# Sums of weights made by accumulating DMAs, and a fourth pair of the gate and up products in sevens

## The chip, the cores and the metric

The kernel runs on one core of a Trainium2 chip. The metric is the device time of one execution in microseconds (us); several executions are timed and the median is compared. Beside the times there is a profile of one execution. The core has TensorE (matmuls, in the profile PE, its weight loads PEld), VectorE (DVE), ScalarE (ACT), GpSimd (POOL) and SyncE (SP), which here issues nearly all DMAs; 16 DMA engines move the data.

## The reference

One decoder layer on 256 tokens of width 2048, in float32: a gated feed-forward half layer, two parallel token mixers, a second feed-forward half layer, and a gated embedding, with a layer norm behind each. The change touches the two feed-forward half layers alone:

```python
def swiglu(x, w_gu, w_down):
    g, u = jnp.split(x @ w_gu, 2, axis=-1)
    return (jax.nn.silu(g) * u) @ w_down

h = layer_norm(alpha * h + 0.5 * swiglu(h, w_ffn1_gu[i], w_ffn1_down[i]), ln_g[i, 0], ln_b[i, 0])
...
h = layer_norm(alpha * h + 0.5 * swiglu(h, w_ffn2_gu[i], w_ffn2_down[i]), ln_g[i, 2], ln_b[i, 2])
```

The inner width is 5632, so the weights of one half layer are 2048 x 11264 (gate and up) and 5632 x 2048 (down), 92 MB and 46 MB.

## The kernel before

**Matmuls in three parts.** Every float32 operand is split into a high part (ScalarE casts it, L90) and a low part (VectorE subtracts, L91). A product is three matmuls of 128x128 against 128x512: low x high, high x high, high x low (`Sum.add`, L286 to L288).

**Weights come in chunks** of 128 x 1024 floats, 512 KB, by one DMA of SP (`Chunk`, L104). For gate and up the columns are taken in 11 blocks j of 512; in a block the 16 rows of 128 inputs form 8 pairs p, and each pair has a chunk for gate (n = 0) and one for up (n = 1). Half a chunk holds the weights of one of the pair's two input rows. For the down product the 44 input rows form 22 pairs, and the output is made in two halves of 2 x 512 columns.

**Singles and sevens.** A pair is a 2 x 2 block product: two halves of the tokens, two input rows, two output columns, so eight products. As two `Single`s it takes 8 products of 3 matmuls, 24 in all. As one `Seven` it takes 7, 21 matmuls, by a scheme of Strassen's kind. For that the four weights b11, b21 (first chunk) and b12, b22 (second chunk) are combined:

- t1 = b11 + b12, t3 = b12 + b22 (tile u; L162, L163)
- t2 = b11 + t3, t4 = t2 + b21 (tile v; L164, L165)

VectorE makes the four sums, each 128 x 512. Then the first chunk, b22, u and v are split into high and low parts, 3.5 tiles of 128 x 1024. The sums of the inputs are made once (`seven_forms`), and `seven_common` folds the four shared results behind a block. The last seven of a block takes its products in another order, so that these results are ready early. In gate and up, the pairs 0, 1 and 2 of blocks 1 to 10 are sevens, block 0 has singles alone: 30 sevens a half layer. In the down product the pairs of four groups are taken: 4 sevens in the first half, 8 in the second.

**The order of the work is written out by a planner.** `plan` lists all singles and sevens in order. `fill()` runs when a unit is done and writes the next instructions: it makes (splits) a loaded unit while less than 45 matmuls of made units stand ahead (`ahead`), and loads the next while less than 90 stand ahead in all (`far`). Each class says how many slots its load takes (`loads`), how many a make needs free (`makes`), how many it keeps (`keeps`), and its matmuls (`time`). A slot is one of 46 tiles of 4 KB a partition that weights share with activations; `slots_for_weights` says how many the weights may have, 24 in most of gate and up, and 18 to 30 in the tight parts of the down product. All engines run this one order; an instruction waits only for its operands and for its slot to be given back. In the before kernel GpSimd has no DMA.

Of the kernel before, what the change touches and what calls it, by code (L numbers as in the profile page):

```python
# [8 lines left out]
F32 = mybir.dt.float32  # L9
# [3 lines left out]
ALU = mybir.AluOpType  # L13
PSUM = bass.MemoryType.PSUM

P = 128
S = 256
# [15 lines left out]
HELD_PAIRS = 3  # L33
SLOTS = 46

SEVEN = (0, 1, 2)

SEVEN_DOWN = (6, 7, 8, 9)

# [8 lines left out]
def layer(ctx: ExitStack, tc: tile.TileContext, io):  # L48
    nc = tc.nc
    sync, act, dve, pool, pe = nc.sync, nc.scalar, nc.vector, nc.gpsimd, nc.tensor  # L50
# [14 lines left out]
    def slot(shape, dt, name):  # L65
        return slots.tile(shape, dt, tag="slot", name=name)
# [8 lines left out]
    def chunk_of(key):  # L75


        name, at = key[0], key[1:]
        if name.endswith("_gu"):
            j, gu, c = at  # L80
            w = io[name][2 * j : 2 * j + 2, gu, c // 2, :, c % 2 * 2 : c % 2 * 2 + 2, :]
            return w.rearrange("g p k n -> p g (k n)")
        if name[-1] == "2":
            j, c = at
            w = io[name[:-1]][j : j + 2, c // 2, :, c % 2 * 2 : c % 2 * 2 + 2, :]
            return w.rearrange("g p k n -> p g (k n)")
        return io[name][at]

    def split(dst_hi, dst_lo, src, lo_engine=None):
        act.copy(dst_hi, src)  # L90
        (lo_engine or dve).tensor_tensor(dst_lo, src, dst_hi, ALU.subtract)  # L91

    class Chunk:
# [18 lines left out]
        def make(self):  # L112
            self.make_hi()
            split(self.hi, self.lo, self.raw)
# [10 lines left out]
    class Single:  # L125


        loads, makes, keeps, time = 1, 2, 2, 12
# [4 lines left out]
        def load(self, **how):  # L133
            self.chunk = Chunk(self.key, **how)
# [4 lines left out]
    class Seven:  # L139
# [1 line left out]

        loads, makes, keeps, time = 2, 6, 7, 21

        def __init__(self, key, other):
            self.key, self.other = key, other

        def load(self):
            self.a, self.b = Chunk(self.key), Chunk(self.other)  # L150

        def make(self):
            a, b = self.a, self.b
            nm = a.name
            b11, b21, b12, b22 = a.of(a.raw, 0), a.of(a.raw, 1), b.of(b.raw, 0), b.of(b.raw, 1)
            u, v = (slot([P, 2, 512], F32, w + nm) for w in "uv")

            def shaped(x):
                return x.rearrange("p (g n) -> p g n", g=2) if a.paired else x

            t1, t3, t2, t4 = (shaped(x) for x in (u[:, 0], u[:, 1], v[:, 0], v[:, 1]))
            dve.tensor_tensor(t1, b11, b12, ALU.add)  # L162
            dve.tensor_tensor(t3, b12, b22, ALU.add)  # L163
            dve.tensor_tensor(t2, b11, t3, ALU.add)  # L164
            dve.tensor_tensor(t4, t2, b21, ALU.add)  # L165

            def parted(name, x):
                hi, lo = (slot([P, 2, 512], F32R, w + name + nm) for w in "hl")
                split(hi, lo, x)
                return [(hi[:, e], lo[:, e]) for e in range(2)]  # L170

            a.make()
            self.b11, self.b21 = a.columns(0), a.columns(1)
            both = slot([P, 2, 512], F32R, "b" + nm)
            self.b22 = both[:, 0], both[:, 1]
            split(shaped(both[:, 0]), shaped(both[:, 1]), b22)
            self.t1, self.t3 = parted("u", u)
            self.t2, self.t4 = parted("v", v)

# [199 lines left out]
    def plan_tokens(key, n_k, nk=2):  # L379
        for c in range(n_k // nk):  # L380
            plan.append(Single(key + (c,)))
# [279 lines left out]
    def gu_units(j):  # L661
        if j == 0:
            return [("P", p) for p in range(KD // 2)]
        plain = [("P", p) for p in range(KD // 2) if p not in SEVEN]
        out = plain[: len(plain) - len(SEVEN)]
        for a, p in zip(SEVEN, plain[len(plain) - len(SEVEN) :]):
            out += [("S", a), p]
        return out

    def gu_keys(name, j):  # L670
        return lambda n, p: (name + "_gu", j, n, p)
# [18 lines left out]
    def plan_ffn(name):  # L690
        for j in range(KF // 4):
            block_units(gu_units(j), gu_keys(name, j))
        first, second, held = down_units()
        block_units(first, down_keys(name, 0))
        block_units(second, down_keys(name, 1))
        plan.extend(Single(down_keys(name, 1)(n, p)) for n in range(2) for p in held)

    def ffn(name, i, ht, norm, keep, residual, keepers, away):
# [27 lines left out]
        for j in range(KF // 4):  # L726
            pg, pu = banks(f"{name}g{j}"), banks(f"{name}u{j}")
            units = gu_units(j)
            plain = len(units) - sum(kind == "S" for kind, p in units)
            n_of = {(0, 0): KD, (0, 1): KD, (1, 0): KD, (1, 1): KD}  # L730
# [13 lines left out]
            def before(u, j=j, offset=KD // 2 - len(units)):  # L744
# [8 lines left out]
                if j == 0 and u == 7:  # L753
                    for g in sorted({p // 2 for p in SEVEN}):
                        hi, lo = (slot([P, 8, P], F32R, f"{name}f{w}{g}") for w in "hl")
# [539 lines left out]
    with tc.manual_schedule():  # L1295
# [8 lines left out]
        for blk in range(4):  # L1304
            plan_tokens(("w_pg", blk), KD)
        kept = sorted({p // 2 for p in SEVEN})
        norm = ffn("f1", 0, ht, None, x_parts, x_columns, (), rows[0])
# [106 lines left out]
```

## Time and profile before

| | us |
|---|---|
| median of 3 runs | 2328.96 (2327.64 to 2329.99) |
| the profiled execution, its own time | 2328.84 |
| its span, first to last instruction | 2327.1 |
| TensorE busy | 2289.2 (98%) |
| VectorE busy | 1828.9 (79%) |
| ScalarE busy | 1145.5 (49%) |
| GpSimd busy | 96.6 (4%) |

How to read it: the times of the groups of instructions are by source line, engine, operation and tile names, where buffer numbers are left out: `rf_gu` is a loaded chunk of gate and up, `hf_gu` and `lf_gu` its parts, `uf_gu` and `vf_gu` the tiles of sums, `huf_gu` and so on their parts, `bf_gu` the parts of b22; `f1` and `f2` stand for the two half layers, and `f14s` for a shared result of block 4 of the first. Matmuls are pipelined, so one that lasts 0.39 us starts less than that behind the last one; the distance of starts counts. In the view by stretches each row has, for one stretch of time, the busy time and count of each engine, the granted clock of TensorE, the share of the DMA engines' time and the GB/s moved. DMA issues are listed with their size and the median time from issue to landing. The two half layers lie at 0 to 690 us and at about 1520 to 2200 us.

### The profile page before, as it was taken

How to read it: one execution, taken by the hardware profiler on the slowest of the kernel's cores; microseconds unless marked ns; L12 is line 12 of the kernel's file. 1: busy time of each engine (PE TensorE's matmuls, PEld its weight loads, DVE VectorE, ACT ScalarE, POOL GpSimd, SP SyncE). 2: the span in 40 equal slices, each digit the busy share in tenths (PEclk: the TensorE clock that was granted, in tenths of full speed). 3: DMA queues.
4: the chain of work that ended last, by engine and by line, in shares of the span. 5: the costliest groups of instructions: out<-in, count | busy, mean ns of one | idle time of the engine just before them, and what ended most of it. 6: DMA issues, size and time to landing. Idle time of an engine off the chain costs nothing.

```text
span 2327.1 us, 28608 instructions
## 1 busy us (share of the span) xinstructions
PE 2289.2 (98%) x10532; PEld 1893.4 (81%) x10532; DVE 1828.9 (79%) x2288; ACT 1145.5 (49%) x1384; POOL 96.6 (4%) x53
## 2 busy tenths in 40 slices
PE   9999999999998999999999999999999999999987
PEld 7888888888887888888778888788888888888876
DVE  7998988988987874777554555769898899889766
ACT  5655555555553343434554443355455555655432
POOL 0000000000000530133000000000000000000000
PEclk9999999999999999999999999999999999999998
DMA  9555665665586564545445666566566666465851
GB/s 316 188 192 186 210 205 171 208 211 193 197 304 239 172 223 160 171 157 189 163 155 181 199 210 215 193 233 211 181 197 201 190 196 219 168 222 199 332 192 55
DMA packets 193725, 465.71 MB, mean 200 GB/s; under 512 B 14768, under 2 KB 16048, under 8 KB 193584
## 3 DMA queue, kind: packets, MB, share of 16 engines
q1 hardware_dynamic: 191456, 460.91, 58.8%
q10 hardware_dynamic: 2128, 2.97, 0.4%
q8 instruction: 83, 1.36, 0.2%
q14 instruction: 58, 0.48, 0.1%
HBM read 455.43 MB, written 8.39 MB: 199 GB/s over the span
## 4 chain that ended last, share of the span: by engine, by line
PE 95%; DVE 4%; DMA 1%; issue 0%; ACT 0%; DVEq 0%; ACTq 0%
PE f1g L286 3%; PE f1g L288 3%; PE f1g L287 3%; PE f2g L286 3%; PE f2g L288 3%; PE f2g L287 3%; PE gt L286 3%; PE f1u L286 3%; PE f1u L288 3%; PE f1u L287 3%; PE rqk L237 3%; PE f2u L287 3%; PE f2u L288 3%; PE f2u L286 3%; PE gt L287 3%; PE gt L288 3%
## 5 line engine op out<-in xcount | busy, mean ns | idle before, releaser
L91 DVE TENSOR_TENSOR lf_gu<-rf_gu,hf_gu 128x1024 fp32r<-128x1024 f32 (+1 forms) x293 | 347.2, 1214 | 23.5 <-ACT hf_gu L90 22.6
L90 ACT CAST hf_gu<-rf_gu 128x1024 fp32r<-128x1024 f32 (+1 forms) x293 | 292.1, 1045 | 16.4 <-DMA rf_gu<-in_f_gu 12.5
L91 DVE TENSOR_TENSOR lw_in_f<-rw_in_f,hw_in_f 128x1024 fp32r<-128x1024 f32 x148 | 208.1, 1438 | 61.8 <-ACT hw_in_f L90 59.2
L91 DVE TENSOR_TENSOR lf_down<-rf_down,hf_down 128x1024 fp32r<-128x1024 f32 x152 | 179.7, 1219 | 20.2 <-ACT hf_down L90 16.8
L90 ACT CAST hf_down<-rf_down 128x1024 fp32r<-128x1024 f32 x152 | 154.5, 1050 | 68.4 <-DMA rf_down<-in_f_down 12.2
L90 ACT CAST hw_in_f<-rw_in_f 128x1024 fp32r<-128x1024 f32 x148 | 145.9, 1052 | 0.2
L90 ACT CAST huf_gu<-uf_gu 128x1024 fp32r<-128x1024 f32 x60 | 63.2, 1054 | 136.7 <-DVE uf_gu L163 133.4
L286 PE MATMUL f1g<-hf_gu,xt 128*128 128x512 f32 x262 | 103.2, 394 | 5.3 <-ACT hf_gu L90 5.3
L288 PE MATMUL f1g<-lf_gu,xt 128*128 128x512 f32 x262 | 102.9, 393 | 0.0
L287 PE MATMUL f1g<-hf_gu,xt 128*128 128x512 f32 x262 | 102.9, 393 | 0.0
L286 PE MATMUL gt<-hw_in_f,ht 128*128 128x512 f32 x256 | 102.5, 400 | 0.0
L286 PE MATMUL f2g<-hf_gu,ht 128*128 128x512 f32 x262 | 102.4, 391 | 0.0
L288 PE MATMUL f2g<-lf_gu,ht 128*128 128x512 f32 x262 | 102.0, 389 | 0.0
L287 PE MATMUL f2g<-hf_gu,ht 128*128 128x512 f32 x262 | 101.9, 389 | 0.0
L287 PE MATMUL gt<-hw_in_f,ht 128*128 128x512 f32 x256 | 99.9, 390 | 0.0
L288 PE MATMUL gt<-lw_in_f,ht 128*128 128x512 f32 x256 | 99.9, 390 | 0.0
L286 PE MATMUL f2u<-hf_gu,ht 128*128 128x512 f32 x232 | 91.5, 394 | 0.0
L286 PE MATMUL f1u<-hf_gu,xt 128*128 128x512 f32 x232 | 91.3, 394 | 0.0
L288 PE MATMUL f2u<-lf_gu,ht 128*128 128x512 f32 x232 | 90.8, 391 | 0.0
L287 PE MATMUL f2u<-hf_gu,ht 128*128 128x512 f32 x232 | 90.6, 391 | 0.0
L287 PE MATMUL f1u<-hf_gu,xt 128*128 128x512 f32 x232 | 90.3, 389 | 0.0
L288 PE MATMUL f1u<-lf_gu,xt 128*128 128x512 f32 x232 | 90.3, 389 | 0.0
(1053 smaller groups left out, 6070.9 us busy)
## 6 DMA issues: line engine op xcount, KB each, us to landing
rf_gu<-in_f_gu SPq DMA_DIRECT2D x351, 512.0 KB, 4.9
rf_down<-in_f_down SPq DMA_DIRECT2D x176, 512.0 KB, 4.5
rw_in_f<-in_w_in_f SPq DMA_DIRECT2D x148, 512.0 KB, 3.7
rw_rv<-in_w_rv SPq DMA_DIRECT2D x32, 512.0 KB, 5.0
rw_ret<-in_w_ret SPq DMA_DIRECT2D x32, 512.0 KB, 4.0
rw_mix<-in_w_mix SPq DMA_DIRECT2D x32, 512.0 KB, 4.3
rw_pg<-in_w_pg SPq DMA_DIRECT2D x32, 512.0 KB, 4.5
rw_att<-in_w_att SPq DMA_DIRECT2D x16, 512.0 KB, 4.2
```

The costliest lines, as they stand in the source:

```text
L90: act.copy(dst_hi, src)
L91: (lo_engine or dve).tensor_tensor(dst_lo, src, dst_hi, ALU.subtract)
L237: pe.matmul(ps[f], hi[:, kk, f * P : (f + 1) * P], rhs(k), start=k == 0, stop=k == n_k - 1,)
L286: pe.matmul(o, al, bh, start=first, stop=False)
L287: pe.matmul(o, ah, bh, start=False, stop=False)
L288: pe.matmul(o, ah, bl, start=False, stop=self.left == 0)
```

## The change

In a seven, t1 and t3 are no longer made by VectorE. SP loads the first chunk as before, copies b12 into both halves of u, and b22 into a third tile x. Then two DMAs of GpSimd add b11 and b22 from HBM onto the halves of u. VectorE makes t2 and t4 as before. b22 is split from x. This holds for the sevens of the down product too. The planner is told that a seven loads into 3 slots and counts as 18 matmuls.

In gate and up, pair 3 becomes a seven as well, in blocks 1 to 10 of both half layers, and the order in a block becomes two pairs of singles, two sevens, a pair, two sevens, a pair.

```diff
-SEVEN = (0, 1, 2)
+SEVEN = (0, 1, 2, 3)
...
-        loads, makes, keeps, time = 2, 6, 7, 21
+        loads, makes, keeps, time = 3, 6, 7, 18
...
         def load(self):
-            self.a, self.b = Chunk(self.key), Chunk(self.other)
-
-        def make(self):
-            a, b = self.a, self.b
-            nm = a.name
-            b11, b21, b12, b22 = a.of(a.raw, 0), a.of(a.raw, 1), b.of(b.raw, 0), b.of(b.raw, 1)
-            u, v = (slot([P, 2, 512], F32, w + nm) for w in "uv")
+            self.a = a = Chunk(self.key)
+            src = chunk_of(self.other)
+            self.u, self.b = (slot([P, 2, 512], F32, w + a.name) for w in "ux")
...
-            t1, t3, t2, t4 = (shaped(x) for x in (u[:, 0], u[:, 1], v[:, 0], v[:, 1]))
-            dve.tensor_tensor(t1, b11, b12, ALU.add)
-            dve.tensor_tensor(t3, b12, b22, ALU.add)
+            self.shaped = shaped
+            (b11, _), (b12, b22) = (
+                [a.of(x, e) for e in range(2)] for x in (chunk_of(self.key), src)
+            )
+            for e in range(2):
+                sync.dma_start(shaped(self.u[:, e]), b12)
+            sync.dma_start(shaped(self.b[:, 0]), b22)
+            pool.dma_start(shaped(self.u[:, 0]), b11, accum_op=ALU.add)
+            pool.dma_start(shaped(self.u[:, 1]), b22, accum_op=ALU.add)
+
+        def make(self):
+            a, u, shaped = self.a, self.u, self.shaped
+            nm = a.name
+            b11, b21 = a.of(a.raw, 0), a.of(a.raw, 1)
+            v = slot([P, 2, 512], F32, "v" + nm)
+            t3, t2, t4 = (shaped(x) for x in (u[:, 1], v[:, 0], v[:, 1]))
             dve.tensor_tensor(t2, b11, t3, ALU.add)
             dve.tensor_tensor(t4, t2, b21, ALU.add)
...
-            split(shaped(both[:, 0]), shaped(both[:, 1]), b22)
+            split(both[:, 0], both[:, 1], self.b[:, 0])
...
         plain = [("P", p) for p in range(KD // 2) if p not in SEVEN]
-        out = plain[: len(plain) - len(SEVEN)]
-        for a, p in zip(SEVEN, plain[len(plain) - len(SEVEN) :]):
-            out += [("S", a), p]
-        return out
+        a, b = list(SEVEN), plain
+        order = "PPSSPSSP"
+        return [("S", a.pop(0)) if kind == "S" else b.pop(0) for kind in order]
```

## The prediction

> **What bounds the kernel now.** I read the page first: the busy times, the strip of the GpSimd engine, the chain that ended last.
>
> ```profile
> span 2327.1 us, 28608 instructions
> PE 2289.2 (98%) x10532; PEld 1893.4 (81%) x10532; DVE 1828.9 (79%) x2288; ACT 1145.5 (49%) x1384; POOL 96.6 (4%) x53
> ...
> POOL 0000000000000530133000000000000000000000
> ...
> PE 95%; DVE 4%; DMA 1%; issue 0%; ACT 0%; DVEq 0%; ACTq 0%
> ```
>
> TensorE is busy 98% of the span and is 95% of the chain: a matmul fewer is time saved, if everything that feeds it keeps up. GpSimd is idle in both feed-forward layers. The view by stretches gives the stages: the start, one gate and up block (170.0 to 212.4), the second half of the down product.
>
> ```profile
> core 0: us, PE busy (x) PEld busy (x) DVE busy (x) ACT busy (x) POOL busy (x), PEclk, DMA share, GB/s
> ...
> 20.00:40.00 20.00, 20.00 (x90) 16.57 (x89) 17.32 (x27) 11.89 (x13) 0.00 (x0) 1.00 1.02 356
> ...
> 170.00:212.40 42.40, 42.40 (x192) 35.18 (x192) 37.68 (x43) 22.91 (x26) 0.00 (x0) 1.00 0.62 198
> ...
> 590.00:690.00 100.00, 100.00 (x443) 82.81 (x442) 88.16 (x100) 52.19 (x55) 0.00 (x0) 1.00 0.69 243
> ```
>
> A block takes 42.4 us, all of it matmuls at full clock, with VectorE at 89% and the DMA engines at 62%. At the start they are full (1.02) at 356 GB/s, so I take 356/1.02 = 349 GB/s as all they can move. The cadence of the matmuls comes from the timeline of TensorE:
>
> ```profile
> 206.07 0.39 PE L286 MATMUL f1g<-hf_gu,xt 128*128 128x512 f32 x1
> ...
> 211.51 0.39 PE L286 MATMUL f14s<-hf_gu,xt 128*128 128x512 f32 x1
> ```
>
> Two singles (24 matmuls) lie between these rows: 5.44/24 = 0.2267 us each.
>
> **The change, part by part.** *Fewer matmuls.* A pair as two singles is 24 matmuls, as a seven 21. One more pair in ten blocks of two layers saves 20 x 3 x 0.2267 = 13.6 us; a block falls from 42.4 to 41.7 us. That is certain; the rest is what may be given back.
>
> *VectorE and ScalarE.* The view of the gate and up tile has their prices:
>
> ```profile
> L104 SPq DMA_DIRECT2D rf_gu<-in_f_gu x351: 367/368/1553, 2.6 to 1950.4; - x176
> L90 ACT CAST hf_gu<-rf_gu x293: 618/1048/1068, 4.6 to 1963.6; 128x1024 fp32r<-128x1024 f32 x146, 128x512 fp32r<-128x512 f32 x1
> L91 DVE TENSOR_TENSOR lf_gu<-rf_gu,hf_gu x293: 691/1218/1228, 5.3 to 1966.7; 128x1024 fp32r<-128x1024 f32 x146, 128x512 fp32r<-128x512 f32 x1
> L90 ACT CAST bf_gu<-rf_gu x60: 609/617/642, 53.7 to 1956.3; 128x512 fp32r<-128x512 f32 x60
> L162 DVE TENSOR_TENSOR uf_gu<-rf_gu,rf_gu x60: 678/684/687, 57.5 to 1958.8; 128x512 f32<-128x512 f32 x60
> L163 DVE TENSOR_TENSOR uf_gu<-rf_gu x60: 679/684/689, 58.1 to 1959.4; 128x512 f32<-128x512 f32 x60
> ```
>
> Each seven loses L162 and L163: 1.37 us of VectorE. A seven then costs it 2 x 0.69 + 3 x 1.22 + 0.68 = 5.7 us, two singles 2.4. Per block: 37.7 - 3 x 1.37 + (5.7 - 2.4) = 36.9 us of 41.7, 88% as before. The order now puts two sevens side by side twice a block: 11.4 us of VectorE against 42 matmuls, 9.5 us. I price that at nothing because the planner makes up to 45 matmuls (10.2 us) ahead; without that cover it would be 1.9 us at each of 40 places. ScalarE gains 3 x 1.05 + 0.62 - 2 x 1.05 = 1.7 us, 24.6 of 41.7: hidden. In the down product, where TensorE never idles, 24 x 1.37 = 33 us less of VectorE is worth nothing.
>
> *DMA volume.* A seven loaded 1.05 MB. Now it loads 0.52 (its first chunk) and three halves of 0.26, and two accumulating DMAs carry 0.26 each from HBM and also read and write the buffer. Per block that is 9.44 MB plain and 2.10 accumulated, against 8.39 now. At 349 GB/s: 27.0 us plus 6.0 us times the price of an accumulated byte. No accumulating DMA is in the trace. At the price of a plain byte the block needs 33.0 us of 41.7 (79%), at twice that, for the extra read, 39.0 (94%). I take twice; then volume alone costs nothing. The halves come in rows of 1 KB where a gate and up chunk has 2 KB:
>
> ```profile
> q1 hardware_dynamic: 191456, 460.91, 58.8%
> q10 hardware_dynamic: 2128, 2.97, 0.4%
> ```
>
> The second queue's packets, 1.4 KB in the mean, took 0.4% x 16 x 2327.1/2128 = 70 ns, 20 GB/s an engine; the first's, 2.4 KB, 114 ns, 21 GB/s. So I price short rows like long ones. SP issues 8 + 4 x 4 = 24 instead of 16, at 0.37 us 8.9 us of 41.7: nothing waits for its issuing. GpSimd's two issues wait for the copies they add to; behind them stand only later accumulations.
>
> *The new wait.* VectorE's first operation of a seven (L164's sum) now waits for copy, then accumulation, in series, and everything later on VectorE stands behind it. So it matters how early loads start. SP waits mostly for slots:
>
> ```profile
> SPq L104 <- PE f1g L288: 157.4, 41, 12.3
> ```
>
> The slot of a load is one that an earlier weight gave back, so a start is tied to a matmul. The tightest place now shows in the down product; rows of SP, VectorE, TensorE:
>
> ```profile
> 557.05 0.80 SPq L104 DMA_DIRECT2D rf_down<-in_f_down  x2
> ```
> ```profile
> 564.77 0.68 DVE L162 TENSOR_TENSOR uf_down<-rf_down,rf_down 128x512 f32<-128x512 f32 x1
> ...
> 566.09 0.69 DVE L164 TENSOR_TENSOR vf_down<-rf_down,uf_down 128x512 f32<-128x512 f32 x1
> ...
> 567.43 1.22 DVE L91 TENSOR_TENSOR lf_down<-rf_down,hf_down 128x1024 fp32r<-128x1024 f32 x1
> ...
> 570.30 1.22 DVE L91 TENSOR_TENSOR lvf_down<-vf_down,hvf_down 128x1024 fp32r<-128x1024 f32 x1
> ```
> ```profile
> 572.72 0.39 PE L286 MATMUL f1d0s<-hf_down,f1al 128*128 128x512 f32 x1
> ...
> 573.17 0.39 PE L288 MATMUL f1d0s<-lf_down,f1ah 128*128 128x512 f32 x1
> ...
> 574.53 0.39 PE L288 MATMUL f1d0s<-lvf_down,f1forms 128*128 128x512 f32 x1
> ```
>
> From the issue to the seven's first matmul are 15.7 us, 69 matmuls: a pair, a seven and a pair, that is, the load took slots that the seven before last gave back. From L164's start VectorE needs 571.52 - 566.09 = 5.4 us to the end of lvf, read at 574.53, and 2.6 us to the end of lf, read at 573.17. So this seven, the last of its half (its products stand in another order), stays on time if the accumulation lands 574.53 - 5.4 - 557.05 = 12.0 us after the first issue; in one that is not last the read of lf decides: 13.5 us.
>
> Where are leads so short after the change? I followed the planner's slot counts in the code, slots given out longest-free first. In each down product five sevens keep 69 matmuls: the third and fourth of the first half, the second to fourth of the second; only one is a last one. In gate and up blocks the fourth seven is the tight one. Each block leaves one more tile in the pool, so its lead shrinks: by my count 99 to 111 matmuls up to block 5, 87 in blocks 6 to 8, and 66 (15.0 us: seven, pair, seven) in 9 and 10, which leaves 12.0 - 0.7 = 11.3 us. The other sevens start 2.7 us earlier or more.
>
> How long is the chain? Rows of DMA issues: the one second load at 557; all in the down product; those at the start, when the engines are full; the spread for the gate and up tile:
>
> ```profile
> rf_down<-in_f_down SPq DMA_DIRECT2D x1, 512.0 KB, 5.7
> ```
> ```profile
> rf_down<-in_f_down SPq DMA_DIRECT2D x68, 512.0 KB, 4.5
> ```
> ```profile
> rf_gu<-in_f_gu SPq DMA_DIRECT2D x14, 512.0 KB, 10.4
> ```
> ```profile
> DMA to landing us min/median/max: 3.3/4.9/13.8
> ```
>
> The second copy is the third issue: 2 x 0.4 + 5.7 = 6.5 us. Two GpSimd issues at SP's 0.37 (a guess from the nearest row): 0.7. The accumulation reads as many bytes as a 512 KB load; bounds 3.3 (the shortest landing) and 10.4 (full engines). With engines near 94% I take the middle of 4.5 and 10.4: 7.4. Chain 14.6 us; bounds 10.5 and 17.6.
>
> [...]
>
> *The sum.* Per layer TensorE waits 4 x (14.6 - 13.5) + (14.6 - 12.0) + 2 x (14.6 - 11.3) = 13.6 us; twice that is 27.2, less the gain of 13.6: +13.6. The profiled execution took 2328.84 us (span 2327.1), the median of the runs is 2328.96: 2328.8 + 13.6 = 2342, and I forecast 2342.
>
> **The rivals.** *All hidden.* If the accumulations land within 5.8 us of their issue, waits stay under 8.9 us and the kernel is faster; with none, 2328.8 - 13.6 = 2315. For it: the landing median 4.5 in the down product; the leads of 87 matmuls and more elsewhere; my starts may err by some 20 matmuls either way. Against: more bytes on the same engines, a second landing in series. [...]
>
> *Eaten up.* Landing between 5.8 and 6.7 us: waits of 8.9 to 18.3 us, within 0.2% of now (4.7 us, about what a measurement of this kernel can tell from no change): 2329.
>
> *The engines full.* If an accumulated byte costs three plain ones, a block needs 27.0 + 18.0 = 45.0 us, 2.6 more than now, x20 = 52; in the down product a seven and a pair take 2.36 MB/349 + 3 x 1.5 = 11.3 us against 45 matmuls, 10.2: x24 = 26. Together about 2407. It decides from 2.6 times a plain byte, (42.4 - 27.0)/6.0. For it: nothing prices the read of the buffer; the loads at the start landed in 10.4 us. Against: the engines have 38% to spare in a block now. [...]
>
> **How the numbers follow.** Forecast (late accumulations, slower by more than they save) 0.42; all hidden 0.33; eaten up 0.10; engines full 0.15. With the accumulation at 10.4 us the chain is 17.6: per layer 4 x 4.1 + 5.6 + 2 x 6.3 + 3 x 1.6 (blocks 6 to 8) = 39.4, in all 2328.8 + 78.8 - 13.6 = 2394. So the likeliest case spans 2334 to 2394, and the range 2314 to 2394 leaves out most of the full engines. Faster 0.33, same 0.10, slower 0.57.
>
> **What would show it.** Right: TensorE's matmuls 10532 - 60 less; blocks at 41.7 us up to 5 and longer in 9 and 10; VectorE waiting for a DMA ahead of L164's sum in the places named; GpSimd's issues landing in 6.7 us or more; L162 and L163 gone and VectorE 88% in a block. Wrong: accumulations that land in 4 to 5 us, or all blocks equally long with the DMA share near 1, or waits in sevens whose leads I called ample.

## The result, and the profile after

The changed kernel takes 2414.44 us (median of 4 runs, 2401.76 to 2420.56) beside 2329.32 us for the kernel before: a ratio of 1.036, 95% interval 1.0315 to 1.0404. The profiled execution took 2401.76 us with a span of 2400.0, 72.9 longer than before. The forecast was 2342, with a range up to 2394: the direction was right, the size was not, and the time lies outside the range.

The page of the changed kernel, the lines that answer to those shown of before:

```profile
span 2400.0 us, 29494 instructions
PE 2310.7 (96%) x10472; PEld 1894.7 (79%) x10472; DVE 1775.6 (74%) x2200; ACT 1166.9 (49%) x1424; POOL 333.3 (14%) x261
...
POOL 1222212201110440133000000012222221011000
...
q1 hardware_dynamic: 241888, 488.18, 61.3%
q0 software_dynamic: 50432, 54.54, 14.4%
...
PE 82%; DMA 8%; DVE 7%; issue 2%; ACT 0%; SPq 0%; POOL 0%; DVEq 0%; POOLq 0%; ACTq 0%
...
uf_gu<-in_f_gu POOLq DMA_DIRECT2D x160, 256.0 KB, 7.7
```

The 60 matmuls are gone (10472). Yet TensorE is busy for longer, 2310.7 us against 2289.2: fewer matmuls took more time. And TensorE fell from 95% to 82% of the chain that ended last, with DMA and VectorE in its place. The waits name the spot (engine, tile, line, what it waited for; total us, times, longest):

```profile
ACT huf_gu L90 <- DMA uf_gu<-in_f_gu: 176.9, 29, 11.4
...
ACT huf_down L90 <- DMA uf_down<-in_f_down: 98.5, 22, 9.8
DVE vf_gu L173 <- DMA uf_gu<-in_f_gu: 92.2, 14, 12.7
...
DVE vf_down L173 <- DMA uf_down<-in_f_down: 38.3, 7, 10.0
```

L173 is the sum that stood in L164 of the kernel before, the first reader of an accumulated half. The mean gate and up block (blocks 3 to 10 of the first half layer, 2 to 10 of the second, 17 in all, from ScalarE's copy of one block's shared result to the same copy in the next) grew from 42.4 to 46.0 us; the second halves of the down product from 100.9 and 101.3 to 110.4 and 109.8, while the first halves shrank by 1.5 and 2.7. 17 x 3.6 = 61 us, so most of the loss is in gate and up. There every place in blocks 3 to 10 where two matmuls start more than 0.7 us apart is at the fourth seven of a block, at its reads of lf and of luf, the low part of t1 and t3.

One place shows the whole mechanism, the fourth seven of block 6. Timelines of SP (L162: the two copies of b12), GpSimd (L164, L165: the accumulations), VectorE and TensorE in the changed kernel (start, duration, instruction; in brackets the idle time before it and what ended it):

```profile
287.35 1.00 SPq L162 DMA_DIRECT2D uf_gu<-in_f_gu  x2
...
289.17 9.20 SPq L104 DMA_DIRECT2D rf_gu<-in_f_gu  x7
```
```profile
295.59 1.22 POOL L164 DMA_DIRECT2D uf_gu<-in_f_gu  x1 [10.41 <-PE f1g L297]
296.58 1.47 POOL L165 DMA_DIRECT2D uf_gu<-in_f_gu  x1
```
```profile
307.39 0.69 DVE L173 TENSOR_TENSOR vf_gu<-rf_gu,uf_gu 128x512 f32<-128x512 f32 x1 [12.68 <-DMA uf_gu<-in_f_gu]
...
308.73 1.22 DVE L91 TENSOR_TENSOR lf_gu<-rf_gu,hf_gu 128x1024 fp32r<-128x1024 f32 x1
```
```profile
305.51 0.39 PE L296 MATMUL f16s<-hf_gu,xt 128*128 128x512 f32 x1
310.00 0.79 PE L297 MATMUL f16s<-lf_gu,xt 128*128 128x512 f32 x1 [4.10 <-DVE lf_gu L91]
...
313.61 0.63 PE L295 MATMUL f16s<-huf_gu,f1fl 128*128 128x512 f32 x1
314.04 0.63 PE L296 MATMUL f16s<-huf_gu,f1fh 128*128 128x512 f32 x1
```

The copies are issued at 287.35; behind them SP issues seven plain loads, the two of the block's last pair and five of the next block; from 295 to 308 us SP's queue takes 83.6% of the 16 engines' time and GpSimd's 25.0%. The second copy is added to from 296.58; the sum lands 10.8 us later, at 307.4, and VectorE has been idle for 12.68 us. The read of lf on TensorE comes 4.1 us late. From the first copy's issue to VectorE's sum are 20.0 us; over the fourth sevens of blocks 3 to 10 of both half layers the median is 18.2 us (14.4 to 20.0).

The second loss stands in the last two rows: 0.43 us from matmul to matmul, where it was 5.44/24 = 0.2267 at full clock in the kernel before. The view by stretches around the same wait has the granted clock (last columns: clock, share of the DMA engines, GB/s):

```profile
300.00:305.00 5.00, 5.00 (x24) 4.14 (x23) 0.00 (x0) 0.00 (x0) 0.00 (x0) 1.00 1.14 290
305.00:310.00 5.00, 0.90 (x5) 0.40 (x4) 2.58 (x4) 2.15 (x3) 0.00 (x0) 0.86 1.01 337
310.00:311.00 1.00, 1.00 (x2) 0.83 (x3) 1.00 (x2) 1.00 (x2) 0.00 (x0) 0.50 0.41 144
...
316.00:320.00 4.00, 4.00 (x20) 3.27 (x19) 3.86 (x7) 0.11 (x1) 1.13 (x2) 1.00 1.12 243
```

The clock is 0.50 for 6.83 us from 308.62 on, and 1.00 again by 316. In the two feed-forward half layers such stretches add up to 58.0 us in the changed kernel, and to none in the kernel before.

### The profile page after: what moved, and what is told of

Its sections match the earlier page's. It is cut to its first block, busy times and chain, and to the rows that moved or that the text cites. A ratio compares the mean times of both kernels' runs of the same rounds, so it can differ in the third digit from the quotient of the medians.

```text
span 2400.0 us, 29494 instructions
## 1 busy us (share of the span) xinstructions
PE 2310.7 (96%) x10472; PEld 1894.7 (79%) x10472; DVE 1775.6 (74%) x2200; ACT 1166.9 (49%) x1424; POOL 333.3 (14%) x261
## 3 DMA queue, kind: packets, MB, share of 16 engines
q1 hardware_dynamic: 241888, 488.18, 61.3%
q0 software_dynamic: 50432, 54.54, 14.4%
## 4 chain that ended last, share of the span: by engine, by line
PE 82%; DMA 8%; DVE 7%; issue 2%; ACT 0%; SPq 0%; POOL 0%; DVEq 0%; POOLq 0%; ACTq 0%
DMA uf_gu<-in_f_gu 5%; PE gt L295 3%; PE rqk L246 2%; PE gt L296 2%; PE gt L297 2%; PE f2g L295 2%; PE f2g L296 2%; PE f2g L297 2%; PE f1g L295 2%; PE f1g L296 2%; PE f1g L297 2%; PE f2u L295 2%; PE f2u L296 2%; PE f2u L297 2%; PE f1u L295 2%
## 5 line engine op out<-in xcount | busy, mean ns | idle before, releaser
L91 DVE TENSOR_TENSOR lf_gu<-rf_gu,hf_gu 128x1024 fp32r<-128x1024 f32 (+1 forms) x273 | 322.8, 1213 | 8.5 <-ACT hf_gu L90 7.7
L90 ACT CAST hf_gu<-rf_gu 128x1024 fp32r<-128x1024 f32 (+1 forms) x273 | 272.8, 1045 | 19.2 <-DMA rf_gu<-in_f_gu 16.0
L164 POOL DMA_DIRECT2D uf_gu<-in_f_gu x80 | 97.1, 1214 | 1138.4 <-DMA rf_gu<-in_f_gu 462.7
L173 DVE TENSOR_TENSOR vf_gu<-rf_gu,uf_gu 128x512 f32<-128x512 f32 x80 | 54.9, 686 | 156.5 <-DMA uf_gu<-in_f_gu 92.2
L90 ACT CAST huf_gu<-uf_gu 128x1024 fp32r<-128x1024 f32 x80 | 84.1, 1051 | 176.9 <-DMA uf_gu<-in_f_gu 176.9
L165 POOL DMA_DIRECT2D uf_gu<-in_f_gu x80 | 119.5, 1494 | 61.5 <-issue 54.7
L90 ACT CAST hvf_gu<-vf_gu 128x1024 fp32r<-128x1024 f32 x80 | 84.2, 1053 | 82.5 <-DVE vf_gu L174 76.7
L295 PE MATMUL f1g<-hf_gu,xt 128*128 128x512 f32 x232 | 92.2, 397 | 5.6 <-ACT hf_gu L90 5.6
L91 DVE TENSOR_TENSOR luf_gu<-uf_gu,huf_gu 128x1024 fp32r<-128x1024 f32 x80 | 97.4, 1218 | 0.0
L91 DVE TENSOR_TENSOR lvf_gu<-vf_gu,hvf_gu 128x1024 fp32r<-128x1024 f32 x80 | 97.4, 1217 | 0.0
L296 PE MATMUL f1g<-hf_gu,xt 128*128 128x512 f32 x232 | 91.7, 395 | 0.0
L295 PE MATMUL f2g<-hf_gu,ht 128*128 128x512 f32 x232 | 91.5, 394 | 0.0
L296 PE MATMUL f2g<-hf_gu,ht 128*128 128x512 f32 x232 | 91.1, 393 | 0.0
```

Source lines behind the costliest of these rows:

```text
L164: pool.dma_start(shaped(self.u[:, 0]), b11, accum_op=ALU.add)
L165: pool.dma_start(shaped(self.u[:, 1]), b22, accum_op=ALU.add)
L295: pe.matmul(o, al, bh, start=first, stop=False)
L296: pe.matmul(o, ah, bh, start=False, stop=False)
```

## The experiments

*Is it the volume?* The accumulations write to a tile that nobody reads.

```diff
-            pool.dma_start(shaped(self.u[:, 0]), b11, accum_op=ALU.add)
-            pool.dma_start(shaped(self.u[:, 1]), b22, accum_op=ALU.add)
+            pool.dma_start(shaped(scratch[:, 0]), b11, accum_op=ALU.add)
+            pool.dma_start(shaped(scratch[:, 1]), b22, accum_op=ALU.add)
```

> As the changed kernel, but the accumulating DMAs add onto a tile that nobody reads, so the sums t1 and t3 lack b11 and b22 (they are the copies of b12); bytes, packets and GpSimd's issues are all there, only VectorE and ScalarE wait for the copies alone. Late chain: no waits of TensorE in the blocks, 41.7 us each, about 2316 to 2325. Engines full: the bytes are the same, blocks of 44 to 50 us as in the changed kernel, 2390 to 2415.

Measured: 2326.63 us, ratio 0.9989 (0.998 to 0.9999). The page, and a block by stretches:

```profile
q0 software_dynamic: 50432, 54.54, 14.8%
```
```profile
170.00:211.70 41.70, 41.70 (x190) 34.62 (x189) 35.57 (x41) 21.17 (x26) 12.96 (x11) 1.00 1.04 276
```

As many packets and bytes as in the changed kernel, but not at the same times. The edit also frees the accumulations from waiting for the copies: GpSimd issues them one behind the other, those of the first half layer from 2 to 423 us, those of the second from 1080 to 1451 us, before that half layer begins. (The tile also takes one of the 46 slots.) So between 170 and 420 us 10 to 12 of them are issued in every 41.7 us, the length of a block, instead of 8, and TensorE is filled with matmuls throughout, at a DMA share of 1.04 to 1.08. There neither the volume nor GpSimd's issuing is what costs, and a share of 1 is not yet a bound. On the second half layer this run says nothing. The run with all three changes, below, has the bytes in their place, and its 17 blocks of both half layers take 41.7 us in the mean. With that the rival of full engines falls for the blocks.

The total is not 2315, since the first block with sevens ended 12 us later than before's. The accumulations fly from 2 us on, beside the loads of the start. The same stretch before, and in this run:

```profile
5.00:60.00 55.00, 54.71 (x228) 44.51 (x229) 46.31 (x71) 30.71 (x36) 0.00 (x0) 1.00 0.94 325
```
```profile
5.00:60.00 55.00, 50.38 (x207) 39.85 (x208) 37.07 (x55) 26.01 (x30) 14.67 (x12) 1.00 1.11 317
```

At a share of 1.11 TensorE is busy for 50.4 of 55 us, and in the changed kernel, with 6 accumulations in this stretch instead of 12, for 54.4. So where the loads alone nearly fill the engines (0.94 before), more bytes most likely do cost.

*Each part alone.* Three sevens a block as before, in the old order, but summed by DMA:

```diff
-SEVEN = (0, 1, 2, 3)
+SEVEN = (0, 1, 2)
...
-        order = "PPSSPSSP"
+        order = "PPSPSPSP"
```

> The sums by DMA alone: three sevens a block in the order of the kernel before, sums by accumulating DMAs in gate and up and in the down product. Theory (late chain: the fourth seven's copy, accumulation and VectorE work in series, about 18 us, come later than TensorE needs them, and each such wait is followed by a stretch at half clock): no two sevens are neighbours and the third one's load starts 20 us or more ahead, so the blocks stay at 42.4 us; the down product keeps its waits (about 9 us in each second half), 2345. Rival (engines full): the block needs 27 + 4.5 x 2 = 36 of 42.4 us of DMA, not full, 2330 to 2345 too. Rival (an accumulating DMA costs wherever it stands, through GpSimd's issue or the engines): blocks of 44 us and more, 2370 or above.

Four sevens in the new order, all sums on VectorE (the kernel before with the two lines of the other edit):

```diff
-SEVEN = (0, 1, 2)
+SEVEN = (0, 1, 2, 3)
...
+        order = "PPSSPSSP"
```

> The fourth seven alone, in the order of the changed kernel, all four sums by VectorE. Both theories: VectorE has 37.7 + 7.1 - 2.4 = 42.4 us of work in a block where TensorE needs 41.7, so VectorE takes over as the bound and the 13.6 us are not gained: 2325 to 2340. No wait for an accumulation, no stretches at half clock.

Measured: 2358.59 (1.0131, 1.0115 to 1.0148) and 2330.37 (1.0006, 0.9997 to 1.0016). With three sevens most gate and up blocks keep their 42.4 us, but the down product, which has the same sevens in both, loses as much as in the changed kernel: 113.6 and 111.5 us in its second halves. That is 14 us more than expected of this run. The rows of one such place in it, a wait of 3.3 us and what follows:

```profile
618.00:622.30 4.30, 1.78 (x8) 1.13 (x6) 1.99 (x3) 1.56 (x2) 0.35 (x1) 1.00 0.85 311
622.30:625.70 3.40, 2.81 (x7) 2.23 (x8) 3.40 (x5) 3.40 (x5) 1.41 (x2) 0.51 0.66 91
```

The fourth seven without the DMA sums gains next to nothing: most blocks of the first half layer take 42.2 us, not 41.7, and its first block with sevens 48.7. A block of 42.2 by stretches:

```profile
176.20:218.40 42.20, 41.96 (x190) 34.48 (x189) 41.61 (x50) 24.37 (x29) 0.00 (x0) 1.00 0.63 198
```

VectorE is busy for 41.61 of 42.20 us. So four sevens in such a block leave VectorE no room, and taking sums off it is a sound idea.

*Is it the chain's length?* SP issues the copies ahead of the first chunk, t3's half first, and GpSimd adds to t3, the half that is read first, ahead of t1:

```diff
-            self.a = a = Chunk(self.key)
...
-            for e in range(2):
+            for e in (1, 0):
                 sync.dma_start(shaped(self.u[:, e]), b12)
-            sync.dma_start(shaped(self.b[:, 0]), b22)
-            pool.dma_start(shaped(self.u[:, 0]), b11, accum_op=ALU.add)
             pool.dma_start(shaped(self.u[:, 1]), b22, accum_op=ALU.add)
+            pool.dma_start(shaped(self.u[:, 0]), b11, accum_op=ALU.add)
+            self.a = Chunk(self.key)
+            sync.dma_start(shaped(self.b[:, 0]), b22)
```

> As the changed kernel, but SP issues the two copies of b12 ahead of the first chunk, and the accumulation for t3, which VectorE reads first, is issued ahead of that for t1. Late chain: the chain of the fourth seven shortens by 2 to 4 us of 18, the waits of TensorE in the blocks halve: 2355 to 2385. Engines full: same bytes, 2400 to 2415.

Measured: 2323.31, ratio 0.9973 (0.9961 to 0.9986), faster than both kernels and far better than expected. The chain of the fourth seven is 13.1 us in the median instead of 18.1; no half clock is left in the feed-forward stages. The same bytes in the same number of DMAs, reordered, were worth 91 us.

Then the two halves of that edit alone. Only the copies ahead of the first chunk, the accumulations in the old order:

```diff
-            self.a = a = Chunk(self.key)
...
             for e in range(2):
                 sync.dma_start(shaped(self.u[:, e]), b12)
-            sync.dma_start(shaped(self.b[:, 0]), b22)
             pool.dma_start(shaped(self.u[:, 0]), b11, accum_op=ALU.add)
             pool.dma_start(shaped(self.u[:, 1]), b22, accum_op=ALU.add)
+            self.a = Chunk(self.key)
+            sync.dma_start(shaped(self.b[:, 0]), b22)
```

> One half of the run that came to 2323.3: the second chunk's copies are issued ahead of the first chunk, but the accumulation of t1 stays ahead of that of t3. The late chain (the fourth seven's accumulation landing about 18 us after its first copy's issue, against a lead of 19.5 us and 3.7 us of work behind it): the copies land some 2 to 3 us earlier, which takes most of a shortfall of 2 to 4 us, and a wait that is left stays short of the 2 us from which TensorE's granted clock halved: 2325 to 2350. If it is the order of the two accumulations that counts, this half alone leaves 2375 to 2400.

Only t3's half first, the first chunk ahead of the copies:

```diff
-            for e in range(2):
+            for e in (1, 0):
...
-            pool.dma_start(shaped(self.u[:, 0]), b11, accum_op=ALU.add)
             pool.dma_start(shaped(self.u[:, 1]), b22, accum_op=ALU.add)
+            pool.dma_start(shaped(self.u[:, 0]), b11, accum_op=ALU.add)
```

> The other half: t3's half is copied and accumulated first, but the first chunk stays ahead of the copies, as in the changed kernel. The first-read sum is then one GpSimd issue of 1.2 us and part of one landing earlier, 1 to 3 us: the late chain gives 2340 to 2385, more than the half with the copies. If the order of the accumulations is what counts: 2325 or below.

Measured: 2341.81 (1.005, 1.0033 to 1.0067) and 2360.56 (1.0139, 1.0112 to 1.0165). Each half gives most of the gain by itself, 73 and 54 us; together they give 91, not 127. The second one moves part of the wait to t1: ScalarE's first cast of both halves now waits for the later of the two, as the waits of that kernel say (the changed kernel had 176.9, so it is hardly less):

```profile
ACT huf_gu L90 <- DMA uf_gu<-in_f_gu: 171.6, 24, 11.5
...
DVE vf_gu L173 <- DMA uf_gu<-in_f_gu: 56.6, 11, 8.4
```

*Or the lead?* The chain is left as it is; only the order within a block differs.

```diff
-        order = "PPSSPSSP"
+        order = "PPSSPPSS"
```

> The chain is left as it is in the changed kernel, and the fourth seven only comes one pair later in the block (pair, pair, seven, seven, pair, pair, seven, seven), which by the planner's rules gives it a lead of 114 matmuls (26 us) where it had 86 (19.5 us). The late chain: with 26 us against 18 + 3.7 the waits at the fourth sevens go, and the half clock with them: 2315 to 2335, though nothing of the DMA work, of GpSimd's issues or of VectorE's sums has changed. If the accumulations cost their time whatever the lead (GpSimd's queue, the engines, or a landing that stretches as far as there is room): 2380 or above.

Measured: 2348.72, ratio 1.0083 (1.0064 to 1.0103). A block by stretches:

```profile
170.00:211.70 41.70, 41.70 (x190) 34.61 (x188) 37.10 (x42) 24.50 (x29) 9.63 (x9) 1.00 1.01 277
```

The chain of the fourth seven is 18.0 us in the median, as long as before, though its parts differ: the accumulation lands in 7.6 us instead of 11.3, but is issued 3.7 us behind the landing of its copy instead of 0.7. Its lead, from the first copy's issue to the seven's first matmul, is 27.5 us in the median of all 20 where the changed kernel has 19.3, and 15 of the 17 blocks counted here take 41.6 to 42.7 us. What the time does not do is reach 2335: the down product, whose order this leaves alone, still has its waits, with second halves of 114.1 and 112.8 us. So the theory holds in the blocks that the edit touches, and the total shows the other place that it applies to.

*Both*, the order of blocks and the reordered chain:

> The longer lead and the shorter chain together. The late chain: no wait is left in the gate and up blocks, so that they come to 41.7 each, 20 blocks by 0.7 us below before = 2315, and at best 2312 with the down blocks as they were in the run with both orders changed: 2312 to 2322. If the second accumulation or the copies then wait for slots, or the down blocks bound it: 2323 and no better than without the longer lead.

Measured: 2318.18, ratio 0.9953 (0.9938 to 0.9968), the best of all. Its page and a block:

```profile
PE 93%; DVE 4%; DMA 2%; ACT 0%; issue 0%; SPq 0%; DVEq 0%; ACTq 0%
...
uf_gu<-in_f_gu POOLq DMA_DIRECT2D x160, 256.0 KB, 8.3
```
```profile
211.70:253.40 41.70, 41.70 (x190) 34.62 (x189) 36.57 (x42) 24.16 (x28) 9.76 (x8) 1.00 1.01 285
```

Its accumulations land in 8.3 us, slower than in the changed kernel (7.7), and it is 96 us faster: what costs is not the landing, but a landing that is later than its reader needs it.

Side by side (the chain is the median from the first copy's issue to the landing that VectorE's sum reads, fourth sevens of blocks 3 to 10; the block is the mean of the 17 defined above; half clock is summed over the feed-forward stages; all in us):

| kernel | chain | block | half clock | median time |
|---|---|---|---|---|
| changed | 18.1 | 46.0 | 58.0 | 2414.44 |
| t3 first | 15.3 | 44.1 | 20.5 | 2360.56 |
| copies first | 16.2 | 43.1 | 6.8 | 2341.81 |
| both of these | 13.1 | 42.6 | 0 | 2323.31 |
| order of the block | 18.0 | 42.1 | 13.7 | 2348.72 |
| all three | 14.1 | 41.7 | 0 | 2318.18 |

The half clock that is left in the fifth row lies in the down product.

*A fifth seven*, on the reordered chain, in two orders:

```diff
-SEVEN = (0, 1, 2, 3)
+SEVEN = (0, 1, 2, 3, 4)
...
-        order = "PPSSPSSP"
+        order = "PPSSSPSS"
```

> A fifth of the eight pairs of a gate and up block goes in sevens, in the order pair, pair, seven, seven, seven, pair, seven, seven, on top of the shorter chain (copies first, t3 first). A look at the volume, which the run with unread accumulations found hidden at four sevens: the engines' busy share in blocks 3 to 10 was 0.61 with three sevens summed on VectorE and 0.99 with four summed by DMA. If that share is time in which the engines could take no more, a fifth seven asks for 0.99 + 0.095 = 1.09 of a block that TensorE would do in 41.0 us, so that a block takes 45 us: 20 x 3 = 60 us above 2318, 2360 to 2400. If the share still has room (it has read 1.14 in a stretch of the changed kernel), only TensorE's work goes, 20 x 0.7 = 13.6 below 2318: 2303 to 2312, with waits at the sevens that have the least lead bringing it to 2330.

```diff
...
-        order = "PPSSPSSP"
+        order = "SSPSSPPS"
```

> The same five sevens in the order seven, seven, pair, seven, seven, pair, pair, seven: the same bytes, instructions and products, other leads. If the engines' volume is the bound it takes the same time as the other order within some 5 us; if the leads are, the two differ by more and the gaps of TensorE stand at the sevens with the least lead.

Measured: 2367.39 (1.0164, 1.0149 to 1.018) and 2484.04 (1.0662, 1.0643 to 1.0681). The two orders differ by 117 us with the same bytes, so what a fifth seven costs is set by the order. In the second the waits of TensorE are not at the sevens, as was expected, but at the transposes that end a block, ahead of which two sevens now start the next one. The waits of TensorE there, then ScalarE in one such place:

```profile
PE f1t L726 <- ACT f1a L728: 63.2, 10, 10.6
...
PE f2t L726 <- ACT f2a L728: 50.6, 10, 8.7
```
```profile
183.52 1.04 ACT L90 CAST huf_gu<-uf_gu 128x1024 fp32r<-128x1024 f32 x1 [7.46 <-DMA uf_gu<-in_f_gu]
184.47 1.04 ACT L90 CAST hvf_gu<-vf_gu 128x1024 fp32r<-128x1024 f32 x1
185.41 0.58 ACT L728 COPY f1a<-f1t 128x512 f32<-128x512 f32 x1
```

In these rows ScalarE's cast of a late sum waits 7.46 us for the accumulation, and the copy that the transposes need (L728), which stands behind it in the program, starts 1.89 us after the cast does: here too an accumulation lands too late, but another instruction pays. The first order came to the 45 us a block that full engines would give, at a share of 1.05, but TensorE has 65 gaps of over 0.5 us between matmuls in its blocks 1 to 10, and the run with unread accumulations had no trouble at 1.04 to 1.08. Whether volume would bind a fifth seven with enough lead stays open.

## Why the prediction was wrong

*The gain of 13.6 us* was right: 60 matmuls less, and blocks of 41.7 us wherever nothing waits. Three changes to order give 2318.18, against the rival "all hidden" at 2315.

*VectorE, ScalarE and SP priced at nothing* was right for the gate and up blocks: with four DMA-summed sevens and no late accumulation VectorE is 36.57 of 41.70 us busy (36.9 had been counted) and TensorE waits for nothing.

*Twice the price for an accumulated byte* was right in the engines' busy time: by the page of the changed kernel, 14.4% x 16 x 2400.0 / 54.54 = 101 us of engine time per MB, against 61.3% x 16 x 2400.0 / 488.18 = 48 for the plain queue, 2.1 times. *The landing of 7.4 us* was right in the median of all accumulations in gate and up (7.7).

*The leads* were wrong, the first step to fail: "99 to 111 matmuls up to block 5, 87 in blocks 6 to 8, and 66 in 9 and 10" came from a hand count of slots. Measured in the changed kernel from the first copy's issue to the fourth seven's first matmul, they are 18.4 to 20.7 us in blocks 1 to 5 of the first half layer (22.4 to 25.2 had been counted), 17.0 to 17.9 in blocks 6 to 8 (19.7), and 19.4 and 17.0 in 9 and 10 (15.0). From the issue of the first chunk, from which the forecast counted, they are 0.5 to 2.0 us longer. So not two blocks of a half layer are tight but nearly all. That was named as a sign of a wrong prediction, "waits in sevens whose leads I called ample".

*The chain of 14.6 us*, bounds 10.5 to 17.6, was the second and weighs more. Counted from the first copy, as here, it is 14.2. With the measured leads less 3.7 us for VectorE's work, that is 13.3 us and more, a chain of 14.2 would have waited 0.9 us at most. The term that was too small is the landing of the accumulation. At the fourth sevens of blocks 3 to 10 the second copy lands in 5.7 us in the median, just as forecast, and the accumulation is issued 0.7 us behind that, as forecast too; but it lands in 11.3 us (5.7 to 12.9) instead of 7.4 (upper bound 10.4). The 7.4 was the middle between a load in the down product and one among full engines. It fits the median accumulation, but the tight seven is not a median one. Four or five plain loads are issued between its first copy and its second accumulation, and at that moment 6 or 7 other DMAs are on their way; at the second and third sevens there are 2 or 3, and their second accumulations land in 5.5 and 5.9 us (at the first sevens 7, and 9.2 us). That these loads are the reason is likely, but no run varies them alone. GpSimd's issues were guessed at 0.37 us and take 1.2 to 1.9 in gate and up, but as the 0.7 us above show, the second issue hardly waits for the first:

```profile
L165 POOL DMA_DIRECT2D uf_gu<-in_f_gu x80: 1194/1624/1882, 44.0 to 2021.7; - x80
```

The 2.6 us from the sum to TensorE's read of lf were right (310.00 - 307.39). With 18.1 us, 20.0 at worst, against 13.3 to 17.0 the waits are some 1 to 5 us.

*What was left out entirely* is the price of a wait. It was taken at its own length. In the trace of the changed kernel waits of some 2 us and more are followed by 3.41 or 6.83 us at half clock, in which a matmul starts every 0.43 us instead of 0.2267. The gaps of TensorE, that is, what the distance of two starts exceeds 0.2267 by where that is over 0.5 us, come to 72.5 us in the changed kernel and 19.8 in the kernel before: 52.7. The half clock is 64.9 us against 10.2 (without the stretch that ends each trace): at most half of the difference, 27.3, is lost; by the distances of the starts within these stretches it is 25.3. 52.7 + 25.3 - 13.6 = 64.4 of the 72.9 us; the other 8 or so are in gaps below 0.5 us and were not split further. Without the half clock the profiled execution would have taken some 2401.8 - 25.3 = 2376 us, inside the range; that is worked out, no run shows it.

*The down product* was predicted rightly in kind, but its size came near by luck: 4 x 1.1 + 2.6 = 7.0 us of waits a layer were forecast, and its two halves together grew by 8.0 and 5.8 us. Of the five sevens that were named the two of the first half did not wait at all: its matmuls take 117.9 us in both kernels. The second and the fourth of the second half waited 1.9 and 5.0 us in the first layer and 2.0 and 2.9 in the second, where 1.1 each was forecast, and half clock followed.

## What to carry to other kernels

A transfer that only starts when another has landed is priced by its lead, as here, and not by its bytes alone: find the consumer with the least lead, and take durations from the moment in which its transfers fly, with what else is on its way then. Put the first link of such a chain ahead of what can wait, and the link that is read first ahead of the others; here that was worth 91 us without a byte less. And look at the granted clock behind a wait: in these traces TensorE's waits cost more than their length once they came to some 2 us in a step of 3.41 us, so that waits just below that were cheap and the same ones a little longer were not.

## What was not expected of the hardware

The half clock came in the same pattern in all twelve traces. The stretches lasted 3.41 us or a multiple (without the one that ends each trace), and their starts lay on a fixed grid of that step: 260.8, 308.6, 359.8 and 407.6 in the changed kernel are 14, 15 and 14 steps apart. I summed TensorE's idle time in each step of that grid in all twelve traces: what the distance of two starts exceeds 0.2267 us by, where that is over 0.2 us. Of the 106 steps with 2.0 us or more idle, all 106 were followed by a step at half clock (with gaps from 0.1 us on counted, 120 of 123). Of 19 with 1.85 to 2.0, 10 were. Of 135 with 1.0 to 1.85, 18 were, and those 18 had run at half clock themselves. Of 246 with 0.3 to 1.0, none was. So in these traces it was not one wait that counted but the idle time within a step: in the step from 356.4 us of the changed kernel 1.3 us of one wait and 0.9 us of another brought it on together. A row pair of the changed kernel, before and behind such a start (clock in the column before the last two):

```profile
255.60:260.80 5.20, 3.35 (x15) 2.37 (x14) 3.23 (x5) 2.81 (x3) 0.00 (x0) 1.00 1.08 370
260.80:267.60 6.80, 6.15 (x16) 4.42 (x15) 6.80 (x7) 5.46 (x7) 3.66 (x3) 0.50 1.12 324
```

That the DMA share stood at 1.04 to 1.08 for whole blocks of the run with unread accumulations, in which TensorE waited for nothing, was not expected either: the forecast had taken a share near 1 as the sign of full engines.
